# Scores kernel: 15 partitions of the last output tile move from SyncE's store to a store on GpSimd's software queue

## The chip, the cores and the metric

One core of one Trainium2 chip runs the kernel. The metric is device time in microseconds, the median of several runs; lower is better. Before the change it is 200.09 us (three runs, 200.01 to 200.18).

## The reference

```python
def reference(q, k):                       # both (8, 8, 512, 64) float32
    scale = 1.0 / np.sqrt(q.shape[-1])
    return (np.einsum('bhqd,bhkd->bhqk', q, k) * scale).astype(np.float32)
```

For each of 8 batches and 8 heads the kernel makes a 512x512 matrix of scaled scores. The inputs are 16.8 MB together, the output is 67.1 MB of float32, so the output is four fifths of what the core moves.

## The kernel before

The output is made in 16 tiles. Tile g is held in SBUF as 128 partitions of 2x8x512 float32 values, which are 32 KB in each partition and 4 MB in all. Four such tiles are kept in `big` (`UNITS` = 4); tile g uses place g % 4. The same memory first receives the inputs.

The work of a tile passes through five engines:

1. SyncE (SP) loads `q` and `k` into `big` at the very start, with eight loads from its queue (lines 72 and 83); half of the first tile of keys comes by ScalarE's queue.
2. GpSimd casts the loaded values to bf16 pairs in `xb` (line 132). It has nothing else to do; its last cast is over by 50 us.
3. VectorE transposes keys and queries, with the queries placed into the zeroed blocks of `qz` (lines 200 and 205).
4. TensorE makes 16 matmuls of 128x128 by 128x512 per tile into the eight banks of PSUM (line 158), in a hardware loop over four tiles.
5. ScalarE scales PSUM into `big`, four banks at a time (line 179); six of the 64 evacuations are VectorE's (line 177). A tile's last evacuation raises the semaphore `out` for every odd tile.

Stores are all issued by SP, in the loop `for g in range(ALL)`. Tiles 0 and 1 have a store of 4 MB each. After that SP waits for `out` after every second tile and stores two tiles at once, 128 partitions of 64 KB (line 89), with `free0` or `free1` as the semaphore; TensorE waits on these two before it starts the tiles that reuse the place. So there are nine stores: two of 4 MB and seven of 8 MB. The last one, for tiles 14 and 15, is issued when tile 15 is evacuated, and nothing is behind it but SP's wait for the two `free` semaphores (lines 108 and 109).

All loads and stores of SP share one hardware queue, spread over the core's 16 DMA engines. An engine takes its packets from that queue one after the other: 32 KB each in the stores, 16 KB in most loads. One 8 MB store is 256 packets, 16 for each engine.

For the last pair, tile 14 lies in place 2 of `big` (`UNITS - 2`) and tile 15 in place 3 (`UNITS - 1`).

## Time and profile before

| | |
|---|---|
| median of the runs | 200.09 us |
| the profiled execution | 200.45 us |
| its span, first to last instruction | 199.1 us |
| outside the span | 1.3 us |
| HBM read, written | 16.78 MB, 67.11 MB |
| mean rate over the span | 421 GB/s |
| busy: VectorE, ScalarE, TensorE, GpSimd | 57%, 53%, 40%, 20% |
| last store issued by SP | at 175.90 us, 0.61 us long |
| SP waits at the end | 22.6 us |

The page gives the share of time in which each engine computes, and a row for DMA: the mean busy share of the 16 DMA engines in each of 40 slices of the span, with the GB/s that they moved. Times called "at" count from the start of the span. In the table by stretches, a DMA packet is counted in the stretch in which it starts, so a stretch can show more than its own length of DMA work. Beside these views, the trace holds a record of each DMA packet (start, length, bytes, queue), though not the number of the engine that carried it.

### The profile page before, as it was taken

Reading aid. Unit: us, or ns where it says so; the run is one execution under the profiler, and the core shown is the slowest. Engines: PE = TensorE matmul, PEld = TensorE weight load, DVE = VectorE, ACT = ScalarE, POOL = GpSimd, SP = SyncE. Lnnn points to the kernel's source line nnn. Section 1 sums busy time; section 2 is a strip of 40 time slices with the busy share of each in tenths; the row PEclk is TensorE's granted clock in tenths of the full one; section 3 lists DMA queues with packets and bytes.
Section 4 is the critical chain, followed back from the end, with each engine's and each line's share of the span. In section 5 each row is a group of like instructions: output and inputs, shape, how many; then the busy total and the mean of one; then the engine's idle time right before and its main releaser. Section 6 shows DMA issues by size and latency. Waiting matters only on the chain.

```text
span 199.1 us, 729 instructions
## 1 busy us (share of the span) xinstructions
PE 79.9 (40%) x256; PEld 23.5 (12%) x256; DVE 113.8 (57%) x61; ACT 105.6 (53%) x59; POOL 38.9 (20%) x20
## 2 busy tenths in 40 slices
PE   0000356546624662565257516550766076600000
PEld 0000011111101110111021102110211021100000
DVE  4238999999478039944993599369926500400000
ACT  2000049949970977197629752974397449730000
POOL 0399999699000000000000000000000000000000
PEclk9999999979995899589957975998599859995555
DMA  6999999999999999999999999999999999999995
GB/s 199 449 431 428 425 421 425 431 438 441 434 428 421 421 421 421 474 441 434 428 428 421 421 430 434 456 434 441 428 428 428 421 421 434 448 441 448 428 428 224
DMA packets 3746, 83.90 MB, mean 421 GB/s; under 512 B 288, under 2 KB 288, under 8 KB 800
## 3 DMA queue, kind: packets, MB, share of 16 engines
q1 hardware_dynamic: 3472, 82.84, 97.2%
q10 hardware_dynamic: 272, 1.05, 1.3%
q14 instruction: 2, 0.02, 0.0%
HBM read 16.78 MB, written 67.11 MB: 421 GB/s over the span
## 4 chain that ended last, share of the span: by engine, by line
DMA 41%; ACT 32%; PE 6%; DVE 4%; POOL 2%; issue 0%; SPq 0%
DMA out_dram<-big 35%; ACT big L179 32%; PE ps L158 6%; DMA big<-in_q_dram 6%; DVE qz L205 4%; POOL xb L132 2%; SPq L89 0%; SPq L107 0%
## 5 line engine op out<-in xcount | busy, mean ns | idle before, releaser
L179 ACT ACTIVATE big<-ps 128x2048 f32<-128x2048 f32 x58 | 104.3, 1888 | 68.3 <-PE ps L158 68.3
L158 PE MATMUL ps<-kT,qz 128*128 128x512 bf16 x256 | 79.9, 450 | 94.0 <-DMA out_dram<-big 35.8
L205 DVE STREAM_TRANSPOSE qz<-xb 32x1024 f32<-32x1024 f32 (+1 forms) x36 | 65.2, 1810 | 1.3 <-POOL xb L132 0.7
L158 PEld LDWEIGHTS ps<-kT,qz 128*128 128x128 bf16 x256 | 23.5, 110 | 149.8 <-ACT big L179 48.7
L132 POOL CAST xb<-big 128x2048 bf16<-128x2048 f32 x16 | 38.7, 2470 | 10.3 <-DMA big<-in_k_dram 7.8
L177 DVE TENSOR_SCALAR big<-ps 128x2048 f32<-128x2048 f32 x6 | 13.8, 2292 | 43.2 <-PE ps L158 43.2
L200 DVE STREAM_TRANSPOSE kT<-xb 64x1024 f32<-64x1024 f32 (+1 forms) x18 | 31.4, 1747 | 11.5 <-POOL xb L132 6.8
L212 DVE MEMSET qz<- 128x4096 uint32 x1 | 3.5, 3472 | 2.9 <-PEq L77 2.9
L179 ACT ACT_TABLE_LOAD x1 | 1.3, 1283 | 2.0 <-PEq L77 2.0
L253 POOL MEMSET const-float32-0.0<- 128x1 f32 x1 | 0.1, 98 | 0.2 <-issue 0.2
L253 POOL MEMSET const-bfloat16-1.0<- 128x1 bf16 x1 | 0.1, 101 | 0.0
L253 POOL MEMSET const-uint8-127<- 128x1 uint8 x1 | 0.1, 101 | 0.0
L253 POOL MEMSET const-float32-1.0<- 128x1 f32 x1 | 0.1, 98 | 0.0
## 6 DMA issues: line engine op xcount, KB each, us to landing
out_dram<-big SPq DMA_DIRECT2D x7, 8192.0 KB
big<-in_q_dram SPq DMA_DIRECT2D x4, 2048.0 KB, 24.2
out_dram<-big SPq DMA_DIRECT2D x2, 4096.0 KB
big<-in_k_dram SPq DMA_DIRECT2D x3, 2048.0 KB, 24.2
big<-in_k_dram ACTq DMA_DIRECT2D x1, 1024.0 KB, 9.0
big<-in_k_dram SPq DMA_DIRECT2D x1, 1024.0 KB, 7.5
```

The source lines that it names most:

```text
L132: cast = nc.gpsimd.tensor_copy(out=dst, in_=src)
L158: ins = pe.matmul(out=ps[:, i], lhsT=qz[:, 2 * t + x, i], rhs=kT[:, 2 * t + x], start=True, stop=True)
L177: freed = nc.vector.tensor_scalar_mul(out=to, in0=src, scalar1=scale)
L179: freed = nc.scalar.mul(out=to, in_=src, mul=scale)
L200: return nc.vector.transpose(out=out, in_=src)
L205: return nc.vector.transpose(out=qw[d:d + Q, b % 2 * G:(b % 2 + 1) * G, rows, h * Q:(h + 1) * Q].rearrange("d g i (m jj) -> d i jj m g", j ...
L212: nc.vector.memset(qz, 0.0).then_inc(sem["zeroed"], 1)
L253: nc = _bacc.Bacc("TRN2", target_bir_lowering=False, num_devices=1)
```

## The change

The last store, of tiles 14 and 15 together, is replaced by four:

- SP stores the whole of tile 14: 128 partitions of 32 KB.
- SP stores partitions 0 to 111 of tile 15.
- SP stores partition 127 of tile 15, its 32 KB written as 16 rows of 2 KB.
- GpSimd stores partitions 112 to 126 of tile 15 from its own, software-made queue.

Ahead of its store GpSimd gets two more instructions, after its last cast: one that sets back a cursor[...], and a load of 5x2x8 values of `q` into a new small tensor `steps`, which nothing reads. The code's intent is that [...]the fifteen-row store lies on engines 5 to 15 and 0 to 3, and not on number 4. GpSimd then waits for `out` to reach 8, as SP does.

The two semaphores `end` and `rest` are new. SP's last wait is for `free0`, for `end` at 48 and for `rest` at 32. Nothing else in the program moves: the instructions of TensorE, VectorE and ScalarE stand in the same order as before, and so do SP's up to the last store.

```diff
+    KEEP = 112
...
+    end_sem = nc.alloc_semaphore("end")
+    rest_sem = nc.alloc_semaphore("rest")
...
+    steps = nc.alloc_sbuf_tensor("steps", [5, 2, 8], f32)[:]
...
-    def store(to, tiles):
-        run = tiles.rearrange("p n x i k -> p n (x i k)")
+    def copy(to, src):
         return nc.sync.add_instruction(mybir.InstDMACopy(
             name=nc.get_next_instruction_name(), engine=mybir.EngineType.SP, mode="Copy",
-            queue="qSPDynamicHW", ins=nc.sync.lower_ap_dma(run), outs=nc.sync.lower_ap_dma(to)))
+            queue="qSPDynamicHW", ins=nc.sync.lower_ap_dma(src), outs=nc.sync.lower_ap_dma(to)))
+
+    def store(to, tiles):
+        return copy(to, tiles.rearrange("p n x i k -> p n (x i k)"))
...
-        else:
+        elif g < ALL - 1:
             store(dst, big[:, g % UNITS - 1:g % UNITS + 1]).then_inc(free, 32)
...
-    for n in range(2):
-        nc.sync.wait_ge(sem[f"free{n}"], 32)
+    last_big, last_dst = big[:, UNITS - 1], dst[:, 2:]
+    store(dst[:, :2], big[:, UNITS - 2:UNITS - 1]).then_inc(end_sem, 16)
+    store(last_dst[:KEEP], big[:KEEP, UNITS - 1:]).then_inc(end_sem, 16)
+    copy(last_dst[P - 1].rearrange("x (i k) -> x i k", i=RO),
+         last_big[P - 1:].rearrange("p x i k -> p (x i) k")).then_inc(end_sem, 16)
+    nc.sync.wait_ge(sem["free0"], 32)
+    nc.sync.wait_ge(end_sem, 48)
+    nc.sync.wait_ge(rest_sem, 32)
...
+    nc.gpsimd.inc_swdge_sem([], [], mode="reset_dge_cursor")
+    nc.gpsimd.dma_start(out=steps, in_=q_r[0, 0:5, 0:2, 0:8]).then_inc(rest_sem, 16)
+    nc.gpsimd.wait_ge(sem["out"], ALL // 2)
+    nc.gpsimd.dma_start(out=last_dst[KEEP:P - 1], in_=last_big[KEEP:P - 1].rearrange(
+        "p x i k -> p x (i k)")).then_inc(rest_sem, 16)
```

## The prediction

> **What bounds the kernel now.** I read the page's busy row first, then the DMA queues, the chain, SP's waits, and last the end of the span in narrow stretches.

> ```profile
> DMA  6999999999999999999999999999999999999995
> ...
> q1 hardware_dynamic: 3472, 82.84, 97.2%
> q10 hardware_dynamic: 272, 1.05, 1.3%
> q14 instruction: 2, 0.02, 0.0%
> ...
> DMA 41%; ACT 32%; PE 6%; DVE 4%; POOL 2%; issue 0%; SPq 0%
> ```

> The DMA row is at 9 from the second slice to the last but one; no engine row is. SP's one queue (q1) is 97.2% of the time of 16 DMA engines. The chain names ScalarE for a third, but only because a store must wait for its tile; the queue has work all the while. So DMA bytes bound the kernel, and only the end of the queue is open to a change of 1 us.

> ```profile
> SPq L109 <- DMA out_dram<-big: 22.6, 1, 22.6
> ```

> SP issues its last store at 175.90 us and then waits 22.6 us: all compute is over, the queue drains.

> ```profile
> core 0: us, PE busy (x) PEld busy (x) DVE busy (x) ACT busy (x) POOL busy (x), PEclk, DMA share, GB/s
> 194.60:195.80 1.20, 0.00 (x0) 0.00 (x0) 0.00 (x0) 0.00 (x0) 0.00 (x0) 0.50 1.01 437
> 195.80:196.70 0.90, 0.00 (x0) 0.00 (x0) 0.00 (x0) 0.00 (x0) 0.00 (x0) 0.50 1.35 583
> 196.70:197.40 0.70, 0.00 (x0) 0.00 (x0) 0.00 (x0) 0.00 (x0) 0.00 (x0) 0.50 0.01 0
> 197.40:197.50 0.10, 0.00 (x0) 0.00 (x0) 0.00 (x0) 0.00 (x0) 0.00 (x0) 0.50 0.77 328
> 197.50:199.10 1.60, 0.00 (x0) 0.00 (x0) 0.00 (x0) 0.00 (x0) 0.00 (x0) 0.50 0.00 0
> ```

> A packet counts where it starts. 583 GB/s over 0.90 us are 525 KB, 16 packets of 32 KB: one for each engine. Then nothing starts for 0.7 us, and then 328 GB/s over 0.10 us: 32.8 KB, one packet. So one engine runs one packet after the other 15 are done. The packet records agree. A 32 KB packet takes 1.2135 us on most engines (27.0 GB/s); followed from packet to packet, one engine averages 1.223 us over some 125 packets, which adds up to 1.2 us. It ends at 198.64 us; the others end between 197.12 and 197.84. Its completion is seen at 199.07 (0.43 us later), and the span ends at 199.12. The mean end of the 16 is 197.48, so perfect balance could win 1.2 us at most.

> [...]

> **The change, part by part.**

> *Bytes.* Before, each engine had 16 packets of the last store. After, all have 8 (tile 14) + 7 (112 partitions), and every engine but number 4 has one of the 15. Number 4 loses one packet, 1.22 us. If number 4 is the slow engine, it ends at 198.64 - 1.22 = 197.42. The next to end is 197.84.

> *Partition 127.* By 16 engines: one 2 KB packet each. The trace has 4 KB packets at 0.159 us; half is 0.08 us. By two engines: 8 x 0.08 = 0.64 us on each. I take 0.08 and keep 0.64 as the other end.

> *SP.* Two more issues of 0.61 us each. They hide behind the 22 us of queued packets; without that cover they'd cost 1.2 us. The final wait gains two semaphores that come before or with the last packet; 0.03 us for one such instruction (28 ns in SP's row), taken as 0. Nothing is queued behind it.

> *GpSimd.* Cursor and small load run after its last cast at 50 us and long before 176: they hide under 125 us of idle time. The wait for `out` has only its store behind it. The store's start-up[...] hides under the 22 us as well[...]. Removing the store's increments of `free1` delays nobody: no tile follows.

> *The 15 packets and the ports.* This term decides. [...]1.2135 becomes 4 x 1.2135 = 4.85 us: 3.64 us lost on each of 15 engines[...].[...] No row of the trace shows ports being shared. Bounds: 0 if engines are not held by ports; 3.64 if in step[...].[...] I take 3.64.

> *The 112 partitions.* If each engine keeps to its port or ports don't matter: 0.[...] I take 0 for the forecast[...] and keep 3.6.

> *Sum.* 197.84 + 3.64 + 0.08 = 201.56 for the last engine; + 0.43 to completion, + 0.05 to the end: span 202.04, against 199.12. That is +2.92 us. The profiled execution would read 200.45 + 2.92 = 203.37; the median stands 0.36 below the profiled execution, so **203.0 us**.

> **The rivals.**

> *Ports don't hold, and number 4 is the slow one (chance 0.28, faster).* Then the end is 197.84 + 0.08 = 197.92, + 0.48 = 198.40: -0.72 us, **199.4**. With two engines for partition 127, a typical one ends at 197.35 + 0.64 = 197.99 (199.4 again), the worst at 198.48 (199.9). For it: the lone packet at 197.4 is real, and all costs but one hide.[...] It decides as long as the loss on the ports is below 0.8 us, the distance 198.64 - 197.84 that number 4 gives up.

> *Ports hold, and the 112 are consecutive too (0.25, slower).* 203.0 + 1.8 to 3.6: **204.8 to 206.6**, middle 205.7.[...] Against it: engines drift apart and then meet less.

> *The change doesn't do what it says (0.12, no change).* The packet records carry no engine number: that number 4 is the slow engine can't be read from them. If it isn't, or the store lands elsewhere, the slow engine keeps 16 packets: +0.08, **200.2**; +0.64 if it is one of the two for partition 127, 200.7[...].

> **How the numbers follow.** Forecast (port sharing in the software store alone) 0.35, its own range 202.0 to 204.3[...]; consecutive 112 too 0.25; ports don't hold 0.28; not as described 0.12. The likeliest is 203.0. The range of 8 in 10 goes from 199.2, just below the faster rival, to 206.0, leaving out part of the 0.25 and the tails. About 0.2% (0.4 us) is what a measurement of this kernel can tell from no change. Slower by more: 0.35 + 0.25 + 0.03 of the last rival's, less 0.02 for a small port effect = 0.61. Faster by more: 0.28 less 0.03 for partition 127's worst case = 0.25. The rest, 0.14, within.

> **What the profile would show.** Forecast right: in the stretch 177 to 184 us the DMA rate drops well below 423 GB/s[...], with packets of 3 to 5 us; after it 27 GB/s per engine again. If the rate also sags in the last 10 us, the 112 partitions share ports. If the faster rival is right, the rate stays at 423 to 437 to the end, packets stay at 1.21 us, and the lone packet at 197.4 is gone. If number 4 isn't slow, a lone packet stays. SP's wait should end on `rest` or `end`, with GpSimd's store landing long before the end. I'd be wrong altogether if GpSimd's store started late, after 190 us, or if other times than the drain moved.

## The result, and the profile after

The changed kernel takes 210.47 us (median of six runs, 208.12 to 211.80) against 200.09 before (six runs, 200.01 to 200.33). Two of the six runs (211.37 and 211.80) lie over 1.5% above the fastest, count as slow and are left out of the comparison: the other four have a median of 209.2 us, 1.046 times as long as before, 95% interval 1.040 to 1.053. The sign was forecast, the size was not: +9.1 us (+10.4 with all six) where +2.9 was predicted, and above the range. The profiled execution is the shortest of the six, 208.12 us, with a span of 206.8 us (before: 200.45 and 199.1).

The page of the changed kernel: its DMA rows and its queues.

```profile
DMA  5999999999999999999999999999999999999992
GB/s 216 444 437 425 428 434 406 415 447 418 450 444 412 425 469 425 406 450 450 418 412 450 439 425 425 452 431 418 437 444 425 418 437 444 409 238 406 323 304 76
...
q1 hardware_dynamic: 3490, 82.35, 94.7%
q0 software_dynamic: 80, 0.49, 1.7%
```

Up to slice 35 of 40 (181 us) no slice stands out against before. In the last five slices the rate is 238, 406, 323, 304 and 76 GB/s, while in all but the very last of them the DMA engines are as busy as ever (9 in the DMA row). Busy and slow: packets take longer. The software queue q0 carries 0.49 MB in 1.7% of the time of 16 engines, 56 us of engine time. At 27.0 GB/s its 491,520 bytes would take 18.2 us. So these packets took three times their time.

SP's waits and GpSimd's DMA issues of the changed kernel (columns of the second: count, KB, us from issue to landing):

```profile
SPq L124 <- DMA out_dram<-big: 28.2, 1, 28.2
```

```profile
out_dram<-big POOLq DMA_DIRECT2D x1, 480.0 KB, 13.7
```

SP waits 28.2 us at the end in place of 22.6. GpSimd's store lands 13.7 us after its issue at 175.7, at 189.5 us, long before the end: it isn't late itself, what comes behind it is.

The same stretches of 3 us for the kernel before and the changed one; the last two columns are the DMA share and GB/s.

```profile
181.00:184.00 3.00, 0.00 (x0) 0.00 (x0) 0.00 (x0) 0.00 (x0) 0.00 (x0) 0.50 0.96 415
193.00:196.00 3.00, 0.00 (x0) 0.00 (x0) 0.00 (x0) 0.00 (x0) 0.00 (x0) 0.50 0.89 382
```

```profile
178.00:181.00 3.00, 0.00 (x0) 0.00 (x0) 0.00 (x0) 0.00 (x0) 0.00 (x0) 0.50 1.03 366
181.00:184.00 3.00, 0.00 (x0) 0.00 (x0) 0.00 (x0) 0.00 (x0) 0.00 (x0) 0.50 1.03 208
184.00:187.00 3.00, 0.00 (x0) 0.00 (x0) 0.00 (x0) 0.00 (x0) 0.00 (x0) 0.50 0.85 279
187.00:190.00 3.00, 0.00 (x0) 0.00 (x0) 0.00 (x0) 0.00 (x0) 0.00 (x0) 0.50 1.05 437
190.00:193.00 3.00, 0.00 (x0) 0.00 (x0) 0.00 (x0) 0.00 (x0) 0.00 (x0) 0.50 1.08 350
193.00:196.00 3.00, 0.00 (x0) 0.00 (x0) 0.00 (x0) 0.00 (x0) 0.00 (x0) 0.50 1.05 339
196.00:199.00 3.00, 0.00 (x0) 0.00 (x0) 0.00 (x0) 0.00 (x0) 0.00 (x0) 0.50 1.03 339
199.00:202.00 3.00, 0.00 (x0) 0.00 (x0) 0.00 (x0) 0.00 (x0) 0.00 (x0) 0.50 0.73 251
202.00:205.00 3.00, 0.00 (x0) 0.00 (x0) 0.00 (x0) 0.00 (x0) 0.00 (x0) 0.50 0.30 115
```

There are two dips, not one. The first, 208 GB/s at 181 to 184 us, lies where GpSimd's 30 packets of 16 KB run among tile 14; by the packet records they take 0.75 to 3.80 us each. At 187 to 190 the full rate is back. Then comes a second sag to 340 GB/s, when the engines go over, one after the other, to the 112 partitions of tile 15. The prediction had the first dip and put the second at nothing.

The packet records, followed from packet to packet, tell three things more. The engines end tile 14 between 188.5 and 194.7 us; before the change they come to the same point within 1.5 us. One engine has no software packet, and it is the slow one: its last 16 packets ahead of 178.9 us average 1.226 us, the next slowest 1.220, most 1.214. So the store does leave out the slow engine. It is the first to end tile 14, at 188.53 us, and yet needs until 201.98 us for its seven packets of the 112 partitions, 13.5 us where seven packets alone take 8.5; one of them takes 3.71 us. The 16 engines end the 112 between 200.28 and 206.31 us. And partition 127 is 16 packets of 2 KB, 0.084 us each, in two chains of eight: two engines, not 16.

### The profile page after: what moved, and what is told of

The parts are those of the page before. It is cut to its first block, busy times and chain, and to the rows that moved or that the text cites. A ratio compares the mean times of both kernels' runs of the same rounds, so it can differ in the third digit from the quotient of the medians.

```text
span 206.8 us, 735 instructions
## 1 busy us (share of the span) xinstructions
PE 80.7 (39%) x256; PEld 23.6 (11%) x256; DVE 113.9 (55%) x61; ACT 105.7 (51%) x59; POOL 40.1 (19%) x22
## 3 DMA queue, kind: packets, MB, share of 16 engines
q10 hardware_dynamic: 272, 1.05, 1.2%
## 4 chain that ended last, share of the span: by engine, by line
DMA 39%; ACT 30%; PE 7%; DVE 4%; POOL 3%; issue 1%; SPq 0%
DMA out_dram<-big 34%; ACT big L202 30%; PE ps L181 7%; DMA big<-in_q_dram 5%; DVE qz L228 4%; POOL xb L148 2%; SPq L93 0%; POOL out_dram L158 0%; SPq L114 0%
## 5 line engine op out<-in xcount | busy, mean ns | idle before, releaser
L158 POOL DMA_DIRECT2D out_dram<-big x1 | 0.6, 560 | 126.0 <-ACT big L202 126.0
L235 DVE MEMSET qz<- 128x4096 uint32 x1 | 3.5, 3472 | 2.9 <-PEq L82 2.9
L156 POOL DMA_DIRECT2D steps<-in_q_dram x1 | 0.7, 695 | 0.0
## 6 DMA issues: line engine op xcount, KB each, us to landing
out_dram<-big POOLq DMA_DIRECT2D x1, 480.0 KB, 13.7
```

What stands on the lines that cost most here:

```text
L156: nc.gpsimd.dma_start(out=steps, in_=q_r[0, 0:5, 0:2, 0:8]).then_inc(rest_sem, 16)
L158: nc.gpsimd.dma_start(out=last_dst[KEEP:P - 1], in_=last_big[KEEP:P - 1].rearrange("p x i k -> p x (i k)")).then_inc(rest_sem, 16)
L235: nc.vector.memset(qz, 0.0).then_inc(sem["zeroed"], 1)
```

## The experiments

The theory, called ports in the prediction and the expectations, is that an engine's packet takes longer when other engines read neighbouring partitions of SBUF at the same time. No trace shows a port, or which partitions would share one: the groupings are the author's assumption, and what the runs measure is the time by the partitions that are read. The rivals are that the software queue is slow by itself, that the crowding is on the HBM side, and that splitting the store costs. The kernel before ran beside each group (200.04 to 200.14 us).

### The parts alone

`e1_split` replaces the last store by one for each of the two tiles:

```diff
     store(dst[:, :2], big[:, UNITS - 2:UNITS - 1]).then_inc(end_sem, 16)
-    store(last_dst[:KEEP], big[:KEEP, UNITS - 1:]).then_inc(end_sem, 16)
-    copy(last_dst[P - 1].rearrange("x (i k) -> x i k", i=RO),
-         last_big[P - 1:].rearrange("p x i k -> p (x i) k")).then_inc(end_sem, 16)
+    store(last_dst, big[:, UNITS - 1:]).then_inc(end_sem, 16)
...
-    nc.gpsimd.inc_swdge_sem([], [], mode="reset_dge_cursor")
-    nc.gpsimd.dma_start(out=steps, in_=q_r[0, 0:5, 0:2, 0:8]).then_inc(rest_sem, 16)
-    nc.gpsimd.wait_ge(sem["out"], ALL // 2)
-    nc.gpsimd.dma_start(out=last_dst[KEEP:P - 1], in_=last_big[KEEP:P - 1].rearrange(
-        "p x i k -> p x (i k)")).then_inc(rest_sem, 16)
```

> Tiles 14 and 15 by two SP stores of 128 partitions each, nothing else of the change. Both theories (ports of SBUF shared; the software queue itself slow): [...]200.1 us as before, within 0.2. If the mere splitting of the store costs, 200.5 or more.

Measured 200.14 us, ratio 0.9999 (0.9991 to 1.0008). The split costs nothing.

`e2_no_tile15` drops the store of tile 15 too.

> Tile 15 isn't stored at all (left out of the output), so eight packets less per engine: the slow engine ends 8 x 1.22 us earlier, 200.1 - 9.8 = 190.3 us. It is the base for the next two; both theories say the same.

Measured 190.42 us, as expected: a base on which a part of tile 15 can be laid.

`e3_soft_consecutive` adds to it GpSimd's two DMAs of the change, unaltered. `e4_soft_stride9` alters the rows:

```diff
-    nc.gpsimd.dma_start(out=last_dst[KEEP:P - 1], in_=last_big[KEEP:P - 1].rearrange(
+    nc.gpsimd.dma_start(out=last_dst[0:P - 1:9], in_=last_big[0:P - 1:9].rearrange(
```

> Tile 14 by SP, and of tile 15 only partitions 112 to 126 by GpSimd's queue (the other 113 are left out). Ports: [...]the latest engine is some 4 to 6 us late against the base: 194.5 to 196.5 us. Software queue slow by itself: the same here. Neither: 190.8 us (one more packet on 15 engines, which the slow one doesn't have).

> As the run with 15 consecutive partitions, but with partitions 0, 9, 18 and so on to 126[...] (the other 113 are left out). Ports: [...]190.8 us, up to 1.2 more[...]. Software queue slow by itself: as late as the consecutive ones, 194.5 to 196.5 us.

Measured 195.18 us (194.80 to 196.23) and 192.52 us (192.32 to 193.48). Same queue, same bytes, 15 rows in both; 2.7 us apart. Stretches of 4 us of the consecutive rows, then of the spread ones:

```profile
180.00:184.00 4.00, 0.00 (x0) 0.00 (x0) 0.00 (x0) 0.00 (x0) 0.00 (x0) 0.50 1.08 233
184.00:188.00 4.00, 0.00 (x0) 0.00 (x0) 0.00 (x0) 0.00 (x0) 0.00 (x0) 0.50 0.97 356
```

```profile
180.00:184.00 4.00, 0.00 (x0) 0.00 (x0) 0.00 (x0) 0.00 (x0) 0.00 (x0) 0.50 1.02 401
184.00:188.00 4.00, 0.00 (x0) 0.00 (x0) 0.00 (x0) 0.00 (x0) 0.00 (x0) 0.50 1.03 438
```

233 against 401 GB/s at about the same busy share. The software packets together take 53.7 us of engine time in `e3` and 23.7 in `e4`, for 18.2 us of bytes at 27.0 GB/s. The spread rows still cost 2.1 us over the base, 0.5 more than the 192.0 us allowed for. At most 1.2 of it is the packet itself; the rest wasn't measured apart.

### SBUF side or HBM side

The two stores differ in where they read and in where they write. `e7` and `e8` cross the two:

```diff
# e7_soft_stride9_to_consecutive
+    nc.gpsimd.dma_start(out=last_dst[KEEP:P - 1], in_=last_big[0:P - 1:9].rearrange(
# e8_soft_consecutive_to_stride9
+    nc.gpsimd.dma_start(out=last_dst[0:P - 1:9], in_=last_big[KEEP:P - 1].rearrange(
```

> GpSimd reads partitions 0, 9, .. 126 of tile 15 and writes them to the 15 consecutive places of the output that belong to partitions 112 to 126, so the values land in other rows than they should; 113 rows are left out. Ports of SBUF: as with stride 9 on both sides, 192.5 us. Crowding on the HBM side: as with consecutive partitions, 195.2 us.

> The reverse: GpSimd reads partitions 112 to 126 and writes them to the places of partitions 0, 9, .. 126, again other rows than they should be, and 113 rows are left out. Ports of SBUF: 195.2 us. HBM side: 192.5 us.

### The 112 partitions alone

`e5_sp_112rows` has tile 14 and the 112 partitions, nothing else of tile 15. `e6_sp_128rows_short` stores as many bytes from all 128:

```diff
-    store(last_dst[:KEEP], big[:KEEP, UNITS - 1:]).then_inc(end_sem, 16)
+    copy(last_dst[:, :, :7 * S], last_big[:, :, :7].rearrange("p x i k -> p x (i k)")).then_inc(end_sem, 16)
```

> Tile 14, then partitions 0 to 111 of tile 15, both by SP; the other 16 partitions are left out and GpSimd stores nothing. Seven packets more per engine than without tile 15 (190.4): 190.4 + 7 x 1.222 = 199.0 us if nothing is shared, which is what a fault of the software queue alone would give. Ports shared by shares of seven consecutive partitions: [...]200.8 to 202.6 us, later if the meetings push each other on.

> The same 3.67 MB by SP, but from all 128 partitions with seven eighths of each row (one eighth of the columns of tile 15 is left out). Ports: [...]199.0 us. If it is the splitting, the byte count or the HBM side that costs, as late as the 112 partitions.

Measured 200.66 us (16 runs, 199.84 to 202.34) and 199.08 us (198.84 to 199.17). 112 partitions cost 1.6 us more than the same bytes from 128, without any software queue. Stretches of 4 us, the 112 first:

```profile
188.00:192.00 4.00, 0.00 (x0) 0.00 (x0) 0.00 (x0) 0.00 (x0) 0.00 (x0) 0.50 1.00 385
192.00:196.00 4.00, 0.00 (x0) 0.00 (x0) 0.00 (x0) 0.00 (x0) 0.00 (x0) 0.50 0.97 352
```

```profile
188.00:192.00 4.00, 0.00 (x0) 0.00 (x0) 0.00 (x0) 0.00 (x0) 0.00 (x0) 0.50 1.02 437
192.00:196.00 4.00, 0.00 (x0) 0.00 (x0) 0.00 (x0) 0.00 (x0) 0.00 (x0) 0.50 0.98 419
```

### The parts together

`e9` puts the spread rows before the 112 partitions, `e10` is the change less partition 127, `e11` replaces its 112 partitions by seven eighths of 128, and `e12` lets SP store the 15 rows:

```diff
# e9_soft_stride9_and_112 (the 112 by SP as in the change)
+    nc.gpsimd.dma_start(out=last_dst[KEEP:P - 1], in_=last_big[0:P - 1:9].rearrange(
# e10_change_without_127
-    copy(last_dst[P - 1].rearrange("x (i k) -> x i k", i=RO),
-         last_big[P - 1:].rearrange("p x i k -> p (x i) k")).then_inc(end_sem, 16)
# e11_soft_consecutive_and_128short, shortened; the new copy is made for x in 0 and 1
-    store(last_dst[:KEEP], big[:KEEP, UNITS - 1:]).then_inc(end_sem, 16)
+    copy(bass.AP(tensor=last_dst.tensor, offset=last_dst[:KEEP, x].offset, ap=[[7 * S, P], [1, 7 * S]]),
+         last_big[:, x, :7].rearrange("p i k -> p (i k)")).then_inc(end_sem, 16)
# e12_all_by_sp, behind the 112, and no GpSimd store
+    store(last_dst[KEEP:P - 1], big[KEEP:P - 1, UNITS - 1:]).then_inc(end_sem, 16)
```

> Tile 14 and 112 partitions of tile 15 by SP, as in the change, but GpSimd reads partitions 0, 9, .. 126 (and writes them to the places of 112 to 126, so wrong rows); partition 127 is left out. If the costs of the two stores add up: 200.7 + (192.5 - 190.4) = 202.8 us. If engines that enter the 112 partitions out of step pay more there, above 203.5.

> The change, with partition 127 left out. If costs add up: 200.7 + (195.2 - 190.4) = 205.5 us, and the rest of 210.5 would be partition 127. If the two stores make each other worse: 208 to 210, and partition 127 is worth at most 1.2 us[...].

> GpSimd's 15 consecutive partitions as in the change, but in place of the 112 partitions SP stores the same bytes from all 128 (seven eighths of each row of tile 15, written to the places of 112 partitions, so values are misplaced and one eighth is left out, partition 127 too). [...]195.2 + 8.6 = 203.8 us. If the late engines were to catch up, less; if the software store alone made up the 210, near 209.

> The change with the 15 partitions stored by SP in place of GpSimd, behind the 112 partitions; whole output, no software queue. Ports: the 112 cost 1.6 and the 15 rows[...] 3.6 more: 200.1 + 1.6 + 3.6 = 205.3 us, up to 206. If the software queue were needed for the loss: 200.1 + 1.6 = 201.7.

Measured 202.94 (three runs; a fourth took 206.93), 211.24, 203.90 and 204.56 us. `e9` adds up (202.8 expected). `e11` adds up: 8.7 us for the bytes of 7 packets behind the software store of `e3`, so late engines stay late but nothing is added while the bytes come from all 128 partitions. `e10` doesn't: 211.24 where 205.5 was the sum. And partition 127 isn't the rest: without it the time is no lower than the change's. `e12`, the same split with no software queue, loses 4.5 us, somewhat less than the 5.2 expected; its last 15 packets take up to 4.23 us where 1.21 is the time alone.

Stretches of 4 us behind the crowded store, the 112 partitions (`e10`) first, then the same bytes from 128 (`e11`):

```profile
192.00:196.00 4.00, 0.00 (x0) 0.00 (x0) 0.00 (x0) 0.00 (x0) 0.00 (x0) 0.50 0.94 303
196.00:200.00 4.00, 0.00 (x0) 0.00 (x0) 0.00 (x0) 0.00 (x0) 0.00 (x0) 0.50 1.00 336
```

```profile
192.00:196.00 4.00, 0.00 (x0) 0.00 (x0) 0.00 (x0) 0.00 (x0) 0.00 (x0) 0.50 0.98 417
196.00:200.00 4.00, 0.00 (x0) 0.00 (x0) 0.00 (x0) 0.00 (x0) 0.00 (x0) 0.50 0.88 376
```

So 5.7 us over the sum belong to the 112 partitions coming behind the crowded store (3.7 by the 209.2 us of the change itself).

### In or out of step

In `e10` the engines leave tile 14 between 188.5 and 193.9 us; in `e9`, which adds up, between 188.5 and 191.0. The new theory is that this is the cause: the late engines meet others in the 112 that they would not have met in step. `e13` is to make eight engines late, by two packets each, without any crowd and without GpSimd: twice eight rows, every fourth partition of 0 to 28 and of 32 to 60, ahead of the 112; `e14` has the same DMAs in the other order.

```diff
# e13; in e14 the first line stands last
-    copy(last_dst[P - 1].rearrange("x (i k) -> x i k", i=RO),
-         last_big[P - 1:].rearrange("p x i k -> p (x i) k")).then_inc(end_sem, 16)
+    copy(last_dst[KEEP:KEEP + 8], last_big[0:29:4].rearrange("p x i k -> p x (i k)")).then_inc(end_sem, 16)
+    copy(last_dst[KEEP + 8:], last_big[32:61:4].rearrange("p x i k -> p x (i k)")).then_inc(end_sem, 16)
     store(last_dst[:KEEP], big[:KEEP, UNITS - 1:]).then_inc(end_sem, 16)
```

> No GpSimd store. Between tile 14 and the 112 partitions SP stores twice eight partitions (0, 4, .. 28 and 32, 36, .. 60 of tile 15, written to the places of 112 to 127, so wrong rows), eight engines with one packet each[...]: these engines come two packets (2.4 us) late into the 112. If coming out of step costs: later than the same DMAs in the other order, by 1 to 4 us (204 to 206 us). If only the software store does harm: as late as in the other order, 202 to 203 us.

> The same DMAs and bytes, but the twice eight partitions come behind the 112, so that all engines enter these in step. 200.7 + 2 x 1.2 = 203.1 us at most, less where the eight engines are not the latest ones; in both theories.

Measured 206.37 us (205.30 to 207.87) and 203.02 us (202.64 to 203.30): the order alone is worth 3.4 us. Stretches of the two, `e13` first:

```profile
192.00:196.00 4.00, 0.00 (x0) 0.00 (x0) 0.00 (x0) 0.00 (x0) 0.00 (x0) 0.50 1.06 344
196.00:200.00 4.00, 0.00 (x0) 0.00 (x0) 0.00 (x0) 0.00 (x0) 0.00 (x0) 0.50 0.53 197
200.00:204.00 4.00, 0.00 (x0) 0.00 (x0) 0.00 (x0) 0.00 (x0) 0.00 (x0) 0.50 0.15 41
```

```profile
192.00:196.00 4.00, 0.00 (x0) 0.00 (x0) 0.00 (x0) 0.00 (x0) 0.00 (x0) 0.50 1.08 401
196.00:200.00 4.00, 0.00 (x0) 0.00 (x0) 0.00 (x0) 0.00 (x0) 0.00 (x0) 0.50 0.56 217
200.00:204.00 4.00, 0.00 (x0) 0.00 (x0) 0.00 (x0) 0.00 (x0) 0.00 (x0) 0.64 0.03 12
```

The opposite attempt, `e15`, keeps the crowded store and brings the engines back into step (all start the 112 at nearly the same time) by a wait:

```diff
     store(dst[:, :2], big[:, UNITS - 2:UNITS - 1]).then_inc(end_sem, 16)
+    nc.sync.wait_ge(end_sem, 16)
+    nc.sync.wait_ge(rest_sem, 32)
     store(last_dst[:KEEP], big[:KEEP, UNITS - 1:]).then_inc(end_sem, 16)
```

> The change with one wait more: SP issues the 112 partitions and partition 127 only when tile 14 and GpSimd's store have landed, so all engines start the 112 in step, with an idle gap of 1 to 2 us for all. Out of step as the cause: 195.2 + about 1.5 + 8.5 + 1.6 + 0.5 = 207.3 us, faster than the change in spite of the wait. Otherwise the gap comes on top: 212 us or more.

Measured 208.91 us (207.79 to 209.12; 1.0425 of the kernel before, 1.040 to 1.045). Against `e10` (1.053, 1.049 to 1.058), which even leaves a row out, that is faster by 2.3 us, although every DMA engine now stands still between 193.9 and 195.5 us. Against the change itself (209.2 us, 1.040 to 1.053) no gain is shown, only that the stop costs nothing there. It is 1.6 us above what was expected, and the packet records show why: all 16 engines start the 112 within 0.27 us of each other, and the stage takes 11.8 us in place of the 10.1 expected (8.5 and 1.6 lost). The engines end their seven packets 9.0 to 11.8 us after the stage begins, 7.4 to 9.7 packet times of 1.2135 us. Which of the 112 partitions each engine reads isn't shown. In `e5` the engines came in 1.3 us apart, and the stage lost 1.6 us in place of 3.3.

### In small software stores

Can bytes be moved to GpSimd's queue in small stores instead? `e16` starts from the kernel before, cuts 4 KB of each partition of tile 13 out of SP's store, and gives them to GpSimd in 32 small stores; `e17` has the cut alone, SP storing the rest as well.

```diff
# e16_own_ports; in e17 the rest is one more SP store of 128 partitions
+            copy(cut_dst[:, :3], cut_run[:, :3]
+                 ).then_inc(free, 16)
+            copy(cut_dst[:, 3, :cut], cut_big[:, 1, 1, :cut]).then_inc(free, 16)
...
+    for n in range(8):
+        o = n // 4 * Q + n % 4
+        soft(slice(o + 20, o + 29, 4))
+        soft(slice(o + 64, o + 93, 4))
+        soft(slice(o, o + 13, 4))
+        nc.gpsimd.dma_start(out=skips[n:n + 1], in_=q_r[0, 0:1, 0, 0:8]).then_inc(rest_sem, 16)
...
```

> The kernel before, whole output, with 4 KB of each partition of tile 13 stored by GpSimd in place of SP, in 32 small stores[...]. Number 4 loses 32 KB, 1.2 us. If its lateness is the engine's and the ports have room: 199.4 to 199.7 us. If its port is what is slow, or small packets cost too much: 200.1 us or more.

> The kernel before, whole output, with the store of tiles 12 and 13 cut by columns into three SP stores of 128 partitions (48 KB, 12 KB and 4 KB of each partition); GpSimd stores nothing. If stores of 128 partitions keep to own ports whatever their columns: 200.1 to 200.4 us, and the loss with the small software stores came from these. If the cut itself breaks the layout: 203 us or more.

Measured 206.21 us (205.11 to 206.65) and 200.36 us (ratio 1.0011, 1.0004 to 1.0018). The cut costs 0.2 us, so the small software stores lose nearly 6. Their data packets are 4 KB at 0.203 us on the mean, and the rows of the last eight stores became 128 packets of 256 B; but the loss is seen in 32 KB packets of SP, which take 2 to 3 us when the last store begins at 178.6 us. What makes them this slow isn't shown, and stays open. No run here with the whole output is faster than the kernel before.

## Why the prediction was right in sign and wrong in size

**Right.** The end of the DMA queue is what the change moves; before 178 us nothing else did. The slow engine is the one without a software packet. SP's further issues hide: `e1` has one more than before, at 0.6 us, and takes 200.14 us. So do GpSimd's steps, whose store lands 17 us ahead of the end. The first term, the 15 packets, was taken at 3.64 us, three packet times more than one alone; the factor was the author's estimate, not read from a trace. `e3` stands 4.76 us above its base, of which the packet itself is some 0.9 (1.21, less the 0.3 us by which the last engine ends behind the next in `e2`). That leaves an estimate of 3.8, near the one made. `e4`, `e7` and `e8` show that it depends on which partitions are read: 192.5 and 192.6 us for every ninth one, 195.7 (and 195.2 in `e3`) for the consecutive ones.

**Wrong: "The 112 partitions ... I take 0 for the forecast", with 3.6 us kept as the other end.** The 3.6, like the 1.8 to 3.6 of the rival with consecutive partitions, was the author's estimate, not read from a trace. That step carries nearly the whole miss. Behind the software store the 112 cost 211.24 - 195.18 = 16.1 us (`e10` less `e3`), where the same bytes from all 128 partitions cost 203.90 - 195.18 = 8.7 (`e11` less `e3`). The term is 7.3 us by `e10`, and 5.3 by the 209.2 us of the change itself. Put in place of 0, it brings +2.9 to between +8.2 and +10.3; measured +9.1. That says where the miss lies and is no second test, since the term is read from kernels that are all but the change. Two errors lie in it. The 0 holds for 128 partitions and not for 112: `e5` against `e6`, 1.6 us. And the two terms were added as if independent. The argument in the prediction against a large value, "engines drift apart and then meet less", fits only a small drift: the stage loses 3.3 us in step (`e15`) and 1.6 with engines 1.3 us apart (`e5`). For a large one it is the wrong way round: `e13` against `e14`, 3.4 us for sixteen rows ahead of the 112 in place of behind. The first term not only costs its own time, it sets the state in which the second is run. That is also why the rival with consecutive partitions, 204.8 to 206.6, put the loss into the right stage and was still too low.

**Small terms.** Partition 127 was taken at 0.08 us with 16 engines, and two engines took it; the last packet of all isn't one of its packets, and `e10` shows no gain without it. The dip was looked for from 177 us; GpSimd's first packet runs at 180.0, which leaves the sum as it is.

**Not settled.** How the meetings add up for a given lateness wasn't worked out: four values were measured (1.6, 3.3, and 5.3 to 7.3 us lost, and 3.4 by order alone). Which partitions hold each other's readers up isn't shown either: of 15 rows only two sets were read, the consecutive ones and every ninth. The runs of the change spread over 3.7 us where the kernel before spreads over 0.3; that fits with an outcome that hangs on small differences of phase, but this was only argued.

## What to carry to other kernels

When the queue is full to the end, as here, a store's price isn't its bytes alone: ask also which partitions are read at the same time (15 consecutive rows cost 2.7 us more than 15 spread ones, `e3` and `e4`), and prefer transfers of all 128 partitions, cut by columns where they must be cut (`e6` and `e17` show no loss or 0.2 us). One packet taken from the slow engine could win 0.7 us at most by the prediction's sum, and the change cost nine, because the 15 rows lay side by side and the 112 left behind lost 5.3 to 7.3 us on top. And when two costs both come from meetings, measure them together: the first changes how the second meets.

## What the runs showed of the hardware that was not expected

- Software packets start late: issued at 175.74 to 176.30 us, the first of the 15 rows runs at 180.02 us, 3.7 us after the end of the issue, in `e4` at 179.97 us as well.
- How far apart the engines come into the 112 partitions matters, and not in one direction: seven packets each lose 3.3 us with starts within 0.27 us (`e15`) and 1.6 us with starts 1.3 us apart (`e5`); sixteen rows ahead of the 112 cost 3.4 us more than the same rows behind (`e13`, `e14`).
- Many small software stores slowed SP's packets: 5.9 us for 0.5 MB (`e16` less `e17`).
